# An encoder block in float32 on one Trainium2 core: 56 low parts of weights by adding transfers, and one more pair by seven products in eight stages

## Chip, core and metric

The kernel runs on one core of a Trainium2 chip. The time is the device time of that core in microseconds (us); lower is better. The other seven cores are idle.

## What is computed

One encoder layer on 256 tokens of width 2048, all in float32: a norm, one wide input projection, two kinds of attention, a gate for each, an output projection, then a gated MLP with a width-3 convolution over the tokens, then an embedding gated by the residual, and a last norm.

```python
h = rms_norm(x, attn_norm)
qa, ka, va, qb, kb, vb, ga, gb = split(h @ w_in)            # 2048 -> 10240
ya = windowed_gqa(qa, ka, va)                               # 8 heads, |i-j| <= 128, sink
yb = dilated_attention(qb, kb, vb)                          # 3 groups of 4 heads
merged = sigmoid(ga) * (ya @ w_branch_a) + sigmoid(gb) * (yb @ w_branch_b)
x = x + merged @ w_out                                      # 2048 x 2048
hf = rms_norm(x, ffn_norm)
g = dwconv(hf @ w_ffn_gate)                                 # 2048 -> 5632
x = x + (gelu(g) * (hf @ w_ffn_up)) @ w_ffn_down            # 5632 -> 2048
gate_p = sigmoid(rms_norm(x, ple_norm) @ w_ple_gate)
x = x + gate_p * (p @ w_ple_proj)
out = rms_norm(x, final_norm)
```

## The kernel before

**Numbers.** Every float32 operand is split into a high part `hi` (a copy to float32r, made by ScalarE, ACT) and a low part `lo = w - hi` (a subtraction by VectorE, DVE). A product of two operands is three matmuls on TensorE (PE): hi*hi, hi*lo, lo*hi. `thirds` issues these three (L408 to L410).

**Weights.** They come as pieces of 128 x 2048 numbers (1 MB) in the order of their use. `load` brings a piece into one of three buffers `raw` by SyncE's queue (SP); `produce` splits it unit by unit into `hi` and `lo`, lines L305 and L306. A unit is mostly 128 x 1024. Units of plain weights go into a ring of six buffers `uh`/`ul`, units of weight sums into a ring of two, `vh`/`vl`. `drop` gives a buffer back when PE has used it and makes `pump` produce the next units. A scheduler then sets the order of the instructions on each engine; instructions under `keep` stay in the order in which the program gives them. Each engine works through its own row strictly in order.

**Stages behind attention.** B0 to B3 (the two gates, each followed by the branch projections ba and bb), D0 and D1 (output projection), E0 and E1 (gate and up of the MLP, one per half of its width), F00, F01, F10, F11 (down projection: first digit the half, second the columns), pp0 and pp1, G0, and G2, G3 (embedding gate). B, D, F and G0 take two chunks of 128 inputs and two blocks of 512 columns at a time. Such a piece is either of kind `s`, eight products of three matmuls (24), or of kind `S` or `Z`, seven products (21) as in Strassen's scheme (in Winograd's form). The seven need sums of weights. For `S`, three DVE operations (L295 to L297) make them in the raw buffer; for `Z` two are enough (L282, L283), since one sum was made before, during the stages E, and laid into main memory: `sum_ahead` loads the parts by GpSimd's queue (POOL, L268), adds on DVE (L271, L272) and stores (L275). The seven also need sums of the activations (`combine`, `sums_of`: five DVE operations and a split). A string per stage says the kind of each piece: `ALT` for B1 to B3, D0, D1 and (with Z for S) G0; `FIRST_GATES` for B0; `DOWN` for the halves of F. `wide_stage` (ba, bb, G2, G3) uses pieces of kind `w`, eight products each.

**Order within a seven-product piece.** Units 0 and 1 are plain (`u`), units 2 and 3 sums (`v`); PE needs unit 2 for its second product. The `v` ring has two buffers, so the sums of one such piece can be split only when PE has left those of the one before. Where two Z stand side by side, the sums of the second are made after its second unit (`behind`).

Of the kernel before, what the change touches and what calls it, by code (L numbers as in the profile page):

```python
# [16 lines left out]
P = 128  # L17
# [74 lines left out]
WIDE = 2 * T  # L92
_JOBS = _plan()
NA = len(_JOBS)
ALT = "SsSsSsSs"
DOWN = ("ZZsZsZsZsZs", "ZsZsZsZsZss")
LASTS = 30
ASK, ADD, STORE = 0, 12, 13
FIRST_GATES = "ssssSsSs"


def _ffn(half):
# [65 lines left out]
def _unit_list():  # L168

    units, of = [], []  # L170
    for p, (kind, _) in enumerate(_PIECES):
        if p == 0:
            cuts = [("n", a * P, b * P) for a, b in ((0, 1), (1, 4), (4, 7), (7, 11), (11, PIECE))]
        elif kind == "Z":
            cuts = [("n", WIDE, 2 * WIDE), ("n", 2 * WIDE, 4 * WIDE), ("T21", 0, 2 * WIDE), ("T03", 2 * WIDE, 4 * WIDE)]
        elif kind == "S":
            cuts = [("n", 0, WIDE), ("n", 2 * WIDE, 4 * WIDE), ("T13", 0, 2 * WIDE), ("T24", 2 * WIDE, 4 * WIDE)]
        else:
            cuts = [("n", 0, 2 * WIDE), ("n", 2 * WIDE, 4 * WIDE)]
# [14 lines left out]
def _encoder(ctx: ExitStack, tc, xt, pt, xrow, cols, gainrow, table, onehot, mask, ident_in, wts, out):  # L194
# [84 lines left out]
    def sums_of_weights(raw):  # L279

        q = [raw[:, i * WIDE:(i + 1) * WIDE] for i in range(4)]
        nc.vector.tensor_tensor(q[1], q[0], q[1], op=ALU.subtract)  # L282
        nc.vector.tensor_tensor(raw[:, 2 * WIDE:], raw[:, 2 * WIDE:], view(q[0], 0, (0, 2), (1, WIDE)), op=ALU.subtract)  # L283

    def produce():

        u = state["unit"]
        p, kind, a, b = _UNITS[u]
        while state["raw"] < min(p + 3, _NPIECES):
            load(state["raw"])  # L290
        raw = raws[p]
        ring = "u" if kind == "n" else "v"
        if kind == "T13":
            q = [raw[:, i * WIDE:(i + 1) * WIDE] for i in range(4)]
            nc.vector.tensor_tensor(raw[:, :2 * WIDE], raw[:, WIDE:3 * WIDE], raw[:, :2 * WIDE], op=ALU.subtract)  # L295
            nc.vector.tensor_tensor(q[2], q[2], q[0], op=ALU.subtract)
            nc.vector.tensor_tensor(q[3], q[3], q[2], op=ALU.subtract)  # L297
        behind = _PIECES[p][0] == "Z" == _PIECES[p - 1][0]
        if kind == "T21" and not behind:
            sums_of_weights(raw)  # L300
        src = raw[:, a:b]
        pool = wpool if ring == "u" else held["tok"]
        hi = pool.tile([P, b - a], FR, name=ring + "h", bufs=RINGS[ring])
        lo = pool.tile([P, b - a], FR, name=ring + "l", bufs=RINGS[ring])
        nc.scalar.activation(hi, src, AF.Copy)  # L305
        nc.vector.tensor_tensor(lo, src, hi.bitcast(F32), op=ALU.subtract)  # L306
        if behind and u == _UNITS_OF[p][1]:
            sums_of_weights(raw)
        made[u] = (hi, lo)
        state["unit"] = u + 1  # L310
        state[ring] -= 1
# [275 lines left out]
    def at(i, f, *a):  # L587

        due.setdefault(i, []).append((f, a))
# [320 lines left out]
    def sums_of(u, tag, s=None):  # L910

        tok = held["tok"]
        f = tok.tile([P, 4, P], F32, name="cmb")
        x11, x21, x12, x22 = (u[:, k, t * P:(t + 1) * P] for k in range(2) for t in range(2))
        nc.vector.tensor_tensor(f[:, 0], x21, x22, op=ALU.add)
        nc.vector.tensor_tensor(f[:, 2], x11, x21, op=ALU.subtract)
        nc.vector.tensor_tensor(f[:, 1], f[:, 0], x11, op=ALU.subtract)
        nc.vector.tensor_tensor(f[:, 3], x12, f[:, 1], op=ALU.subtract)
        if s is None:
            s = tok.tile([P, 2, 4, P], FR, name="S", tag="S%d" % tag)  # L920
        nc.scalar.activation(s[:, 0], f, AF.Copy)
        nc.vector.tensor_tensor(s[:, 1], f, s[:, 0].bitcast(F32), op=ALU.subtract)
        return s
# [36 lines left out]
        return h  # L960

    at(("B0", 3, 0), open_tok)
    for i, when in ((4, (3, 1)), (6, (3, 6)), (0, (5, 2)), (2, (7, 2))):
        at(("B0", *when), combine, "hs", hs, i, i // 2)
    rh = halved(rc[0])

    for j in range(4):

        def gated(t, n, a):
            c = held["c"][t][:, cut[n]]  # L970
            nc.vector.tensor_tensor(c, a, c, op=ALU.add)
            a = c
            nc.scalar.activation(c, a, AF.Tanh, scale=rh[:, t:t + 1])

        if j == 1:
            at(("ba1", 0, 0), combine, "merged", held["merged"], 0, 4)
        if j == 3:
            at(("B3", 2, 4), combine, "merged", held["merged"], 2, 0)
            at(("B3", 4, 4), combine, "merged", held["merged"], 4, 1)
        quads("B%d" % j, lambda k: hs[:, k, :], lambda i: combos["hs", i], gated)  # L980
        if j == 0:
            held["merged"] = big.tile([P, KC, 2 * T], FR, name="merged", tag="R1")
        c = held["c"]
        for half, (stage, y, names) in enumerate((("ba%d" % j, lambda k: ya[:, k, :], ("M1", "M6")), ("bb%d" % j, yb.get, ("M7", "M5")))):
            accs = wide_stage(stage, y, names)
            for t in range(2):
                m = c[t][:, cut[half]]
                nc.vector.scalar_tensor_tensor(m, m, 1.0, accs[t], op0=ALU.add, op1=ALU.mult)
                if half:
                    nc.vector.tensor_tensor(c[t][:, cut[0]], c[t][:, cut[0]], m, op=ALU.add)  # L990
        merged_turns("B%d" % (j + 1) if j < 3 else "D0", j, c)
# [7 lines left out]
    def residual(stage, s, moving, key, square):  # L999

        wide = slice(2 * s * WIDE, 2 * (s + 1) * WIDE)

        def finish(t, n, a):
            r = xr[:, t, cut[2 * s + n]]
            nc.vector.tensor_tensor(r, r, a, op=ALU.add)
            if n:
                nc.vector.tensor_tensor(xr[:, t, wide], xr[:, t, wide], held["c"][t], op=ALU.add)
            if n and square:
                nc.scalar.activation(held["c"][t], xr[:, t, wide], AF.Square,
                                     accum_out=held["ssq"][:, s, t:t + 1])  # L1010

        quads(stage, moving, lambda i: combos[key, i], finish)
# [127 lines left out]
    for half in range(2):  # L1140
        held["act"], held["places"] = {}, places(half)
        jobs = _ffn(half)
        joint = 0 if half else JOINT
        stage = "E%d" % half
        accs = [bank(which) for which in ("M1", "M5", "M6", "M7")[:joint]]
        if joint:
            products(stage, lambda k: hf[:, k, :], KC, accs)
        for (kind, n), a in zip(jobs, accs):
            mlp(kind, n, a)
        turns["e"] = 0  # L1150
        todo = [(p, h) for p in sevens(half) for h in range(2)]
# [12 lines left out]
        residual("F%d0" % half, 0, activation_row, "act", half)
        if half:
            pl = big.tile([P, KC, 2 * T], FR, name="pl", tag="R0")
            for pair, when in enumerate((("F11", 0, 6), ("F11", 1, 2), ("F11", 1, 5), ("F11", 2, 1))):
                at(when, rows_pair, "P22", pair, pl, 2)
            at(("F11", 2, 4), combine, "pl", pl, 0, 0)
            at(("F11", 4, 4), combine, "pl", pl, 2, 1)  # L1170
        residual("F%d1" % half, 1, activation_row, "act", half)


# [8 lines left out]
        held["rp"] = halved(rows_root())  # L1182

    at(("pp1", 0, 0), ple_root)
    at(("pp1", 0, 4), combine, "pl", pl, 4, 2)
    at(("G0", 1, 4), combine, "pl", pl, 6, 3)
    names = ("M1", "M6", "M7", "M5")

    class Rows:
# [118 lines left out]
```

## Time and profile before

| | |
|---|---|
| time of three runs, median (lowest to highest) | 1455.31 us (1454.77 to 1455.72) |
| span of the profiled execution, first to last instruction | 1453.7 us, 19747 instructions |
| busy: PE, DVE, ACT, POOL | 1442.7 (99%), 1220.8 (84%), 829.6 (57%), 73.8 us (5%) |
| DMA | 310.17 MB, mean 213 GB/s |
| mean granted TensorE clock | 0.997 |

The profiled execution has no time of its own beside its span; the median of the runs lies 1.6 us above the span. PE's matmuls overlap, so busy time says that PE was never long without one, and the distance from start to start says what one costs. A time in a row counts from the start of the span. In the rows of groups, what stands after the bar is busy time, the mean duration of one in ns, and the idle time of the engine just before.

### The profile page before, as it was taken

Reading aid. Unit: us, or ns where it says so; the run is one execution under the profiler, and the core shown is the slowest. Engines: PE = TensorE matmul, PEld = TensorE weight load, DVE = VectorE, ACT = ScalarE, POOL = GpSimd, SP = SyncE. Lnnn points to the kernel's source line nnn. Section 1 sums busy time; section 2 is a strip of 40 time slices with the busy share of each in tenths; the row PEclk is TensorE's granted clock in tenths of the full one; section 3 lists DMA queues with packets and bytes.
Section 4 is the critical chain, followed back from the end, with each engine's and each line's share of the span. In section 5 each row is a group of like instructions: output and inputs, shape, how many; then the busy total and the mean of one; then the engine's idle time right before and its main releaser. Section 6 shows DMA issues by size and latency. Waiting matters only on the chain.

```text
span 1453.7 us, 19747 instructions
## 1 busy us (share of the span) xinstructions
PE 1442.7 (99%) x7470; PEld 1234.0 (85%) x7470; DVE 1220.8 (84%) x1730; ACT 829.6 (57%) x1148; POOL 73.8 (5%) x113
## 2 busy tenths in 40 slices
PE   9999999999999999999999999999999999999997
PEld 8888888888888888888888888888888888888885
DVE  7677665679998989989877999997878799998994
ACT  7455544546555656566545566465545466555753
POOL 0000000000000000000221100000121200000000
PEclk9999999999999999999999999999999999999998
DMA  9753445435456456465767655566776765556462
GB/s 330 252 209 146 155 167 175 172 143 203 189 190 231 180 210 239 178 253 203 277 238 267 241 208 198 189 248 227 263 275 243 271 236 213 197 194 233 173 236 82
DMA packets 58522, 310.17 MB, mean 213 GB/s; under 512 B 7028, under 2 KB 12020, under 8 KB 29500
## 3 DMA queue, kind: packets, MB, share of 16 engines
q1 hardware_dynamic: 49388, 280.46, 53.1%
q0 software_dynamic: 8320, 27.27, 5.2%
q8 instruction: 58, 0.95, 0.3%
q10 hardware_dynamic: 720, 1.19, 0.2%
q14 instruction: 36, 0.29, 0.1%
HBM read 299.94 MB, written 8.95 MB: 212 GB/s over the span
## 4 chain that ended last, share of the span: by engine, by line
PE 98%; DMA 0%; issue 0%; DVE 0%; ACT 0%; SPq 0%; POOLq 0%; POOL 0%; DVEq 0%
PE bank L351 29%; PE bank L358 15%; PE bank L408 15%; PE bank L409 14%; PE bank L410 14%; PE bank L397 2%; PE bank L399 2%; PE bank L398 2%; PE bank L335 2%; PE bank L336 1%; PE bank L939 1%; PE bank L755 0%; PE bank L703 0%; PE bank L702 0%; PE bank L701 0%; DMA raw<-in_wts 0%
## 5 line engine op out<-in xcount | busy, mean ns | idle before, releaser
L305 ACT ACTIVATE uh<-raw 128x1024 fp32r<-128x1024 f32 (+2 forms) x519 | 518.1, 1010 | 297.0 <-PE bank L410 106.5
L306 DVE TENSOR_TENSOR ul<-raw,uh 128x1024 fp32r<-128x1024 f32 (+2 forms) x519 | 594.4, 1164 | 96.5 <-ACT uh L305 65.9
L351 PE MATMUL bank<-hf,uh 128*128 128x512 f32 x1408 | 336.3, 391 | 0.0
L351 PEld LDWEIGHTS bank<-hf,uh 128*128 128x128 f32 x1408 | 258.9, 188 | 50.1
L358 PEld LDWEIGHTS bank<-hf,ul 128*128 128x128 f32 x1408 | 180.4, 191 | 6.7
L358 PE MATMUL bank<-hf,ul 128*128 128x256 f32 x1408 | 182.8, 283 | 0.0
L305 ACT ACTIVATE vh<-raw 128x1024 fp32r<-128x1024 f32 x96 | 101.1, 1058 | 59.8 <-DVE raw L282 27.0
L306 DVE TENSOR_TENSOR vl<-raw,vh 128x1024 fp32r<-128x1024 f32 x96 | 116.3, 1220 | 1.1
L351 PE MATMUL bank<-hs,uh 128*128 128x512 f32 x432 | 103.6, 392 | 0.0
L351 PEld LDWEIGHTS bank<-hs,uh 128*128 128x128 f32 x432 | 79.5, 188 | 15.6
L410 PE MATMUL bank<-uh,act 128*128 128x512 f32 x218 | 84.9, 390 | 0.0
L409 PE MATMUL bank<-ul,act 128*128 128x512 f32 x218 | 84.8, 389 | 0.0
L408 PE MATMUL bank<-uh,act 128*128 128x512 f32 x218 | 84.6, 390 | 0.0
L496 ACT ACTIVATE t<-bank 128x256 f32<-128x256 f32 x122 | 45.3, 374 | 59.8 <-PE bank L358 48.7
L408 PE MATMUL bank<-uh,hs 128*128 128x512 f32 x172 | 67.4, 392 | 0.0
L410 PE MATMUL bank<-uh,hs 128*128 128x512 f32 x172 | 67.2, 391 | 0.0
L409 PE MATMUL bank<-ul,hs 128*128 128x512 f32 x172 | 67.0, 389 | 0.0
L1084 ACT ACTIVATE gw<-gw,cl 128x256 f32<-128x256 f32 x44 | 24.0, 594 | 72.2 <-DVE gw L1081 71.9
L271 DVE TENSOR_TENSOR ahead<-ahead 128x256 f32<-128x256 f32 x52 | 21.9, 422 | 46.8 <-DMA ahead<-in_wts 46.8
L268 POOL DMA_DIRECT2D ahead<-in_wts x52 | 39.0, 750 | 375.7 <-DMA ahead<-ahead 207.0
L358 PE MATMUL bank<-hs,ul 128*128 128x256 f32 x432 | 56.6, 284 | 0.0
L358 PEld LDWEIGHTS bank<-hs,ul 128*128 128x128 f32 x432 | 54.5, 191 | 1.0
(266 smaller groups left out, 2423.8 us busy)
## 6 DMA issues: line engine op xcount, KB each, us to landing
raw<-in_wts SPq DMA_DIRECT2D x225, 1024.0 KB, 4.9
ahead<-in_wts POOLq DMA_DIRECT2D x52, 384.0 KB, 5.2
raw<-in_wts SPq DMA_DIRECT2D x26, 768.0 KB, 5.1
ahead<-ahead POOLq DMA_DIRECT2D x52, 128.0 KB, 4.4
raw<-ahead SPq DMA_DIRECT2D x26, 256.0 KB, 4.9
raw<-in_wts SPq DMA_DIRECT2D x12, 512.0 KB, 7.0
xr<-in_xrow SPq DMA_DIRECT2D x4, 512.0 KB, 8.4
x<-in_xt SPq DMA_DIRECT2D x13, 128.0 KB, 6.0
```

What stands on the lines that cost most here:

```text
L268: keep(nc.gpsimd.dma_start(q, wts[p][:, :3 * WIDE].rearrange("p (q c) -> p q c", c=WIDE)[:, :, cols]))
L305: nc.scalar.activation(hi, src, AF.Copy)
L306: nc.vector.tensor_tensor(lo, src, hi.bitcast(F32), op=ALU.subtract)
L335: nc.tensor.matmul(acc, hi[:, w], m, start=first, stop=False, skip_group_check=True)
L351: nc.tensor.matmul(acc, weights(u)[0][:, o * P:(o + 1) * P], m, start=first, stop=False, skip_group_check=True)
L358: nc.tensor.matmul(acc[:, T:], weights(u)[1][:, o * P:(o + 1) * P], m[:, :T], start=False, stop=last, skip_group_check=True)
L397: nc.tensor.matmul(acc[:, :n * P], xh, hi, start=(k == 0), stop=False)
L398: nc.tensor.matmul(acc[:, :n * P], xh, lo, start=False, stop=False)
L408: nc.tensor.matmul(acc, sh, wh, start=first, stop=False)
L409: nc.tensor.matmul(acc, sh, wl, start=False, stop=False)
L410: nc.tensor.matmul(acc, sl, wh, start=False, stop=last)
L496: keep(nc.scalar.activation(t, acc[:, T:], AF.Copy, scale=scale))
```

## The change

**Low parts by adding transfers.** `_MOVED` is a set of 56 units: the second unit of each piece of kind `s` or `w` in B, ba, bb, D, F and G0 (27 in B, ba and bb, 6 in D, 20 in F, 3 in G0). For them ACT makes two copies, `-hi` into the low buffer and `hi`; then a transfer issued by POOL reads the same 512 KB of weights from main memory once more and adds them to the low buffer. The DVE subtraction falls away. The transfer is under `keep`.

**One more pair by seven products** in each of B1, B2, B3, D0, D1, G0, F10 and F11, by the strings. Some pieces by seven now stand side by side (`SS`, `ZZ`), and `behind` holds for S too. B0 keeps two, at later places. `combine` is asked for one more pair in each of hs, merged and pl, at new places, and the added sums get a buffer `act2`. G0's third Z and F1's sixth make six more sums ahead, 34 in E1 where there were 28.

```diff
-ALT = "SsSsSsSs"
-DOWN = ("ZZsZsZsZsZs", "ZsZsZsZsZss")
+ALT = "SsSSsSSs"
+DOWN = ("ZZsZsZsZsZs", "ZZsZsZsZsZs")
-FIRST_GATES = "ssssSsSs"
+FIRST_GATES = "sssssSSs"
...
+_MOVED = {_UNITS_OF[p][1] for stage in _STAGES if stage[0] in "BbDFG" and stage not in ("G2", "G3")
+          for p in _STAGES[stage] if _PIECES[p][0] in 'sw'}
...
-        if kind == "T13":
-            q = [raw[:, i * WIDE:(i + 1) * WIDE] for i in range(4)]
-            ...
-        behind = _PIECES[p][0] == "Z" == _PIECES[p - 1][0]
+        behind = _PIECES[p][0] in "SZ" and _PIECES[p - 1][0] in "SZ"
+        if kind == "T13" and not behind:
+            all_sums_of_weights(raw)
...
-        nc.scalar.activation(hi, src, AF.Copy)
-        nc.vector.tensor_tensor(lo, src, hi.bitcast(F32), op=ALU.subtract)
+        if u in _MOVED:
+            nc.scalar.activation(lo, src, AF.Copy, scale=-1.0)
+            nc.scalar.activation(hi, src, AF.Copy)
+            keep(nc.gpsimd.dma_start(lo, wts[p][:, a:b], accum_op=ALU.add))
+        else:
+            nc.scalar.activation(hi, src, AF.Copy)
+            nc.vector.tensor_tensor(lo, src, hi.bitcast(F32), op=ALU.subtract)
         if behind and u == _UNITS_OF[p][1]:
-            sums_of_weights(raw)
+            (sums_of_weights if _PIECES[p][0] == "Z" else all_sums_of_weights)(raw)
...
-    for i, when in ((4, (3, 1)), (6, (3, 6)), (0, (5, 2)), (2, (7, 2))):
-        at(("B0", *when), combine, "hs", hs, i, i // 2)
+    for i, when, tag in ((5, (3, 6), 2), (6, (4, 5), 3), (0, (5, 5), 0), (2, (6, 5), 1), (3, (7, 2), 5)):
+        at(("B0", *when), combine, "hs", hs, i, tag)
```

In the built program PE has 24 matmuls of 128x512 fewer. How the rows stand at the places that matter, the numbers behind a name telling one buffer from another:

ACT near the start of F01, before: the second unit of the fourth piece (an `s`), which PE uses against `act1`, is `uh_8631`; it stands behind the sums `vh_8615` of the Z ahead of it.

```order
L305 ACTIVATE vh_8549<-raw_8405 128x1024
L305 ACTIVATE uh_8590<-raw_8481 128x1024
L305 ACTIVATE vh_8561<-raw_8405 128x1024
L305 ACTIVATE vh_8605<-raw_8481 128x1024
L305 ACTIVATE uh_8621<-raw_8565 128x1024
L305 ACTIVATE vh_8615<-raw_8481 128x1024
L305 ACTIVATE uh_8631<-raw_8565 128x1024
L305 ACTIVATE uh_8663<-raw_8575 128x512
```

The same place now: the second unit of that piece is `uh_8730`, and its negative copy `ul_8731`, on which the adding transfer waits, stands one row further back.

```order
L316 ACTIVATE vh_8647<-raw_8502 128x1024
L316 ACTIVATE uh_8689<-raw_8579 128x1024
L316 ACTIVATE vh_8659<-raw_8502 128x1024
L312 ACTIVATE ul_8670<-raw_8544 128x1024
L316 ACTIVATE vh_8704<-raw_8579 128x1024
L316 ACTIVATE vh_8714<-raw_8579 128x1024
L316 ACTIVATE uh_8720<-raw_8663 128x1024
L313 ACTIVATE uh_8730<-raw_8663 128x1024
L312 ACTIVATE ul_8731<-raw_8663 128x1024
```

So the transfer can start only behind both copies, which both stand behind the sums `vh_8714` of the Z.

DVE at the end of E1, before: rows of L500 gather E1's products out of the PSUM banks (the last three are `bank_11252`, `bank_11314` and `bank_11361`), which F10's products then take; L282 and L283 make the sums of F10's first Z (`raw_11172`), L306 splits weights.

```order
L282 TENSOR_TENSOR raw_11172<-raw_11172 128x512
L283 TENSOR_TENSOR raw_11172<-raw_11172 128x1024
L1092 SCALAR_TENSOR_TENSOR gw_11143<-gw_11143 128x512
L500 TENSOR_TENSOR pair_11191<-bank_11252,t_11306 128x256
L306 TENSOR_TENSOR vl_11299<-raw_11172,vh_11298 128x1024
L306 TENSOR_TENSOR vl_11303<-raw_11172,vh_11302 128x1024
L1101 SCALAR_TENSOR_TENSOR pair_11191<-pair_11191,rms_5806 128x512
L306 TENSOR_TENSOR ul_11342<-raw_11220,uh_11341 128x1024
L1102 TENSOR_TENSOR pair_11191<-pair_11191,gw_10933 128x512
L306 TENSOR_TENSOR ul_11354<-raw_11220,uh_11353 128x1024
L1111 TENSOR_TENSOR act1_11311<-pair_11191,act1_11311 128x2x256
L500 TENSOR_TENSOR pair_11357<-bank_11314,t_11358 128x256
```

The same place now; the last three products are `bank_11387`, `bank_11459` and `bank_11509`, F10's first Z is `raw_11301` and its second `raw_11354`:

```order
L284 TENSOR_TENSOR raw_11301<-raw_11301 128x512
L285 TENSOR_TENSOR raw_11301<-raw_11301 128x1024
L1104 SCALAR_TENSOR_TENSOR gw_11272<-gw_11272 128x512
L317 TENSOR_TENSOR vl_11433<-raw_11301,vh_11432 128x1024
L317 TENSOR_TENSOR vl_11437<-raw_11301,vh_11436 128x1024
L273 TENSOR_TENSOR ahead_11328<-ahead_11328 128x256
L511 TENSOR_TENSOR pair_11323<-bank_11387,t_11443 128x256
L274 TENSOR_TENSOR ahead_11328<-ahead_11328 128x256
L1113 SCALAR_TENSOR_TENSOR pair_11323<-pair_11323,rms_5899 128x512
L317 TENSOR_TENSOR ul_11488<-raw_11354,uh_11487 128x512
L1114 TENSOR_TENSOR pair_11323<-pair_11323,gw_11059 128x512
L317 TENSOR_TENSOR ul_11500<-raw_11354,uh_11499 128x1024
```

The gather of the third last product stood ahead of the splits of the Z's sums; now it stands behind them and behind an addition for a sum ahead (L273), which waits for a load. From there to the gather of the next product it is 14 rows, where it was 7: the second Z's splits and sums and the sums of one pair of activations.

POOL before, behind attention: nothing but two norms until the sums ahead of E0.

```order
L528 TENSOR_TENSOR rr_595<-rv_593,mhalf_78 128x4
L528 TENSOR_TENSOR rr_5757<-rv_5755,mhalf_78 128x2
L268 DMA ahead_5996<-in_wts 128x3x256
L268 DMA ahead_6045<-in_wts 128x3x256
L275 DMA ahead152_5995<-ahead_5996 128x256
L268 DMA ahead_6098<-in_wts 128x3x256
```

POOL now, at the end of E1: the last sums ahead, and right behind them the adding transfers for F10.

```order
L277 DMA ahead247_11014<-ahead_11114 128x256
L270 DMA ahead_11228<-in_wts 128x3x256
L277 DMA ahead248_11227<-ahead_11228 128x256
L270 DMA ahead_11328<-in_wts 128x3x256
L277 DMA ahead248_11227<-ahead_11328 128x256
L314 DMA ul_11586<-in_wts 128x1024
L314 DMA ul_11647<-in_wts 128x1024
L314 DMA ul_11727<-in_wts 128x1024
```

All 33 adding transfers of the stages B and D stand on POOL in front of its first load for a sum ahead; in F no other work stands between them.

More of the change, by code (lines that the diff above doesn't have):

```diff
@@ L283, in sums_of_weights, with all_sums_of_weights @@
         nc.vector.tensor_tensor(raw[:, 2 * WIDE:], raw[:, 2 * WIDE:], view(q[0], 0, (0, 2), (1, WIDE)), op=ALU.subtract)
+    def all_sums_of_weights(raw):
+        q = [raw[:, i * WIDE:(i + 1) * WIDE] for i in range(4)]
+        nc.vector.tensor_tensor(raw[:, :2 * WIDE], raw[:, WIDE:3 * WIDE], raw[:, :2 * WIDE], op=ALU.subtract)
+        nc.vector.tensor_tensor(q[2], q[2], q[0], op=ALU.subtract)
+        nc.vector.tensor_tensor(q[3], q[3], q[2], op=ALU.subtract)
     def produce():
@@ L292, in produce @@
         ring = "u" if kind == "n" else "v"
-        if kind == "T13":
-            q = [raw[:, i * WIDE:(i + 1) * WIDE] for i in range(4)]
-            nc.vector.tensor_tensor(raw[:, :2 * WIDE], raw[:, WIDE:3 * WIDE], raw[:, :2 * WIDE], op=ALU.subtract)
-            nc.vector.tensor_tensor(q[2], q[2], q[0], op=ALU.subtract)
-            nc.vector.tensor_tensor(q[3], q[3], q[2], op=ALU.subtract)
-        behind = _PIECES[p][0] == "Z" == _PIECES[p - 1][0]
+        behind = _PIECES[p][0] in "SZ" and _PIECES[p - 1][0] in "SZ"
+        if kind == "T13" and not behind:
+            all_sums_of_weights(raw)
         if kind == "T21" and not behind:
@@ L919, in sums_of @@
         if s is None:
-            s = tok.tile([P, 2, 4, P], FR, name="S", tag="S%d" % tag)
+            s = tok.tile([P, 2, 4, P], FR, name="S", tag="S%d" % tag if tag < 5 else "act2")
         nc.scalar.activation(s[:, 0], f, AF.Copy)
@@ L978, in _encoder @@
             at(("B3", 2, 4), combine, "merged", held["merged"], 2, 0)
-            at(("B3", 4, 4), combine, "merged", held["merged"], 4, 1)
+            at(("B3", 4, 4), combine, "merged", held["merged"], 3, 1)
+            at(("B3", 7, 4), combine, "merged", held["merged"], 5, 5)
         quads("B%d" % j, lambda k: hs[:, k, :], lambda i: combos["hs", i], gated)
@@ L1170, in _encoder @@
             at(("F11", 4, 4), combine, "pl", pl, 2, 1)
+            at(("F11", 6, 4), combine, "pl", pl, 3, 2)
         residual("F%d1" % half, 1, activation_row, "act", half)
@@ L1184, in _encoder @@
     at(("pp1", 0, 0), ple_root)
-    at(("pp1", 0, 4), combine, "pl", pl, 4, 2)
-    at(("G0", 1, 4), combine, "pl", pl, 6, 3)
+    at(("pp1", 0, 4), combine, "pl", pl, 5, 3)
+    at(("G0", 1, 4), combine, "pl", pl, 6, 4)
     names = ("M1", "M6", "M7", "M5")
```

## The prediction

> **What bounds the kernel now.** I read the page first: the busy line, the chain that ended last and the DMA rate in forty slices.
>
> ```profile
> PE 1442.7 (99%) x7470; PEld 1234.0 (85%) x7470; DVE 1220.8 (84%) x1730; ACT 829.6 (57%) x1148; POOL 73.8 (5%) x113
> PE 98%; DMA 0%; issue 0%; DVE 0%; ACT 0%; SPq 0%; POOLq 0%; POOL 0%; DVEq 0%
> GB/s 330 252 209 146 155 167 175 172 143 203 189 190 231 180 210 239 178 253 203 277 238 267 241 208 198 189 248 227 263 275 243 271 236 213 197 194 233 173 236 82
> ```
>
> PE carries the whole chain, so only two things change the time: matmuls taken away, and matmuls that come to wait. The waits say how many wait now (total us, count, largest).
>
> ```profile
> PE bank L234 <- DVE mhalf L229: 1.1, 1, 1.1
> PE bank L336 <- DVE ul L306: 0.2, 1, 0.2
> ACT uh L305 <- DMA raw<-in_wts: 41.5, 35, 3.0
> DVE ahead L271 <- DMA ahead<-in_wts: 46.8, 25, 3.3
> POOL ahead L268 <- DMA ahead<-ahead: 207.0, 48, 5.6
> ```
>
> PE's two waits come to 1.3 us. There is no stall that relief of DVE could give back: what DVE saves is worth nothing by itself, what PE loses counts in full. ACT already waits for 35 weight loads, DVE for 25 loads of the sums ahead. The windows by stage show the room that is left (window, us, PE, PE load, DVE, ACT, POOL busy with counts, clock, DMA share, GB/s): B1, D0, D1, F01.
>
> ```profile
> 367.00:425.00 58.00, 58.00 (x261) 47.95 (x260) 54.07 (x65) 34.31 (x38) 0.00 (x0) 1.00 0.53 195
> 542.00:585.00 43.00, 43.00 (x194) 35.25 (x193) 41.74 (x51) 26.92 (x29) 0.00 (x0) 1.00 0.68 248
> 585.00:627.00 42.00, 42.00 (x189) 33.42 (x189) 40.28 (x49) 25.59 (x33) 0.00 (x0) 1.00 0.52 193
> 930.00:987.00 57.00, 57.00 (x252) 46.78 (x251) 54.08 (x58) 31.37 (x34) 0.00 (x0) 1.00 0.61 226
> ```
>
> DVE is busy 93 to 97% of these stages though 84% overall, ACT some 60%. So the change relieves the engine that is nearly full, in the right stages; its price is paid in latency and DMA traffic.
>
> **The change, part by part.** *24 matmuls less.* Two matmuls twelve apart stand 2.75 us apart, 0.229 us each.
>
> ```profile
> 1295.45 0.39 PE L408 MATMUL bank<-uh,act 128*128 128x512 f32 x1
> 1298.20 0.39 PE L408 MATMUL bank<-vh,S 128*128 128x512 f32 x1
> ```
>
> 24 x 0.229 = **-5.5 us**, all on the path. This is the floor: nothing else shortens PE's row.
>
> *Busy time of DVE, ACT and POOL.* The durations are those of the groups:
>
> ```profile
> L306 DVE TENSOR_TENSOR ul<-raw,uh 128x1024 fp32r<-128x1024 f32 x466 | 560.9, 1220 | 81.6 <-ACT uh L305 51.4 <-PE bank L358 15.5 <-issue 13.7
> L305 ACT ACTIVATE uh<-raw 128x1024 fp32r<-128x1024 f32 x466 | 486.0, 1054 | 236.0 <-PE bank L351 80.8 <-PE bank L410 71.8 <-DMA raw<-in_wts 39.1
> L306 DVE TENSOR_TENSOR ul<-raw,uh 128x512 fp32r<-128x512 f32 x49 | 33.7, 687 | 12.7 <-ACT uh L305 12.4
> L283 DVE TENSOR_TENSOR raw<-raw 128x1024 f32<-128x1024 f32 x26 | 31.7, 1220 | 0.2
> L282 DVE TENSOR_TENSOR raw<-raw 128x512 f32<-128x512 f32 x26 | 17.9, 687 | 0.2
> L295 DVE TENSOR_TENSOR raw<-raw 128x1024 f32<-128x1024 f32 x22 | 26.9, 1222 | 0.3
> L296 DVE TENSOR_TENSOR raw<-raw 128x512 f32<-128x512 f32 x22 | 15.1, 685 | 0.0
> L918 DVE TENSOR_TENSOR cmb<-pair,cmb 128x128 f32<-128x128 f32 x23 | 6.6, 285 | 0.1
> L922 DVE TENSOR_TENSOR S<-cmb,S 128x512 fp32r<-128x512 f32 x16 | 11.0, 685 | 0.0
> L268 POOL DMA_DIRECT2D ahead<-in_wts x52 | 39.0, 750 | 375.7 <-DMA ahead<-ahead 207.0 <-PE bank L410 168.7
> L271 DVE TENSOR_TENSOR ahead<-ahead 128x256 f32<-128x256 f32 x52 | 21.9, 422 | 46.8 <-DMA ahead<-in_wts 46.8
> ```
>
> DVE loses 56 x 1.22 = 68 us. A new S adds splits of 0.69 + 1.22 and sums of 1.22 + 2 x 0.685, 4.5 us; a new Z the same splits and sums of 0.69 + 1.22, 3.8 us; five S and three Z make 34. Four more combinations are 4 x (5 x 0.285 + 0.685) = 8, six more sums ahead 6 x 2 x 0.422 = 5. DVE stands 21 us better over the whole. ACT gets 56 x 1.05 = 59 us, covered by its 236 us of idle time ahead of these copies; POOL 56 x 0.75 = 42, covered since it has nothing else there. The place where that cover fails is the latency of single units.
>
> *Latency of a moved low part, F.* Before, the low part is ready one subtraction (1.22 us) behind the copy. Now it is ready one more copy and one transfer later. No row shows an adding transfer. The nearest are POOL's own loads (KB, median us to landing), and the spread of a tile's landings (weights, then sums ahead):
>
> ```profile
> raw<-in_wts SPq DMA_DIRECT2D x225, 1024.0 KB, 4.9
> ahead<-in_wts POOLq DMA_DIRECT2D x52, 384.0 KB, 5.2
> ahead<-ahead POOLq DMA_DIRECT2D x52, 128.0 KB, 4.4
> DMA to landing us min/median/max: 2.7/5.0/8.9
> DMA to landing us min/median/max: 3.3/4.8/6.5
> ```
>
> POOL's two sizes give 0.8 us for 256 KB, so 5.6 us for 512 KB as a plain load and 7.2 if the target is read as well, like 1 MB. I take the middle, 6.4 us; the ends are 3.3 (POOL's fastest) and 8.9 (the slowest of all). How much lead there is now, from the copy to the first matmul that takes its low part, I followed unit by unit behind attention. Most have 8 us and more. The tight ones, one each in F00, F01 and F11, are the second unit of a plain piece behind the sums of a Z (copies of ACT, then PE; the first copy of a row ends 1.04 us after its start):
>
> ```profile
> 889.57 2.52 ACT L305 ACTIVATE uh<-raw 128x1024 fp32r<-128x1024 f32 x3
> 895.54 0.39 PE L409 MATMUL bank<-ul,act 128*128 128x512 f32 x1
> 947.07 2.51 ACT L305 ACTIVATE uh<-raw 128x1024 fp32r<-128x1024 f32 x3
> 951.63 0.39 PE L409 MATMUL bank<-ul,act 128*128 128x512 f32 x1
> 1310.16 2.51 ACT L305 ACTIVATE uh<-raw 128x1024 fp32r<-128x1024 f32 x3
> 1315.70 0.39 PE L409 MATMUL bank<-ul,act 128*128 128x512 f32 x1
> ```
>
> Leads 4.93, 3.52 and 4.50 us. The extra copy takes 0.95 (three copies start within 2.5 us), which leaves 3.98, 2.57 and 3.55. At 6.4 the low parts come 2.4, 3.8 and 2.9 us late: **+9**. At 3.3 only F01's does, 0.7: +1; at 8.9 it is 4.9 + 6.3 + 5.4: +17. The order agrees that nothing was pulled forward: in F01 the copy that the transfer waits for still stands behind the sums `vh_8714`.
>
> The Trainium skill ("DMA: Bandwidth & Descriptors", "Anatomy of one DMA — SWDGE (gpsimd) path") fits a transfer issued from GpSimd by 2.0 us + bytes/436e3, an estimate of 3.2 us for 512 KB, and the F term would be under 1 us. The same formula gives 2.9 us for the 384 KB load, where this trace has 5.2, so in this loaded kernel the trace disagrees with it.
>
> *Start of F10, by E1's last gathers.* PE needs the banks that E1's last products leave. The last gather and the first matmul in the bank it frees:
>
> ```profile
> 1234.73 0.42 DVE L500 TENSOR_TENSOR pair<-bank,t 128x256 f32<-128x256 f32 x1
> 1235.78 0.39 PE L408 MATMUL bank<-uh,S 128*128 128x512 f32 x1
> ```
>
> It ends at 1235.15, 0.63 us before its use. In the new order seven more DVE rows stand between the last gathers (0.4 to 1.22 each, some 6 us), and an addition for a sum ahead stands in front, which waits 1.9 us in the mean (46.8/25), 3.3 at most. Behind it, in DVE's row, wait gathers, and PE behind those. The bounds are 0, if DVE, relieved, runs that far ahead, and 6 + 1.9 - 0.6 = 7. I take **+4**, the middle.
>
> *D0 and D1.* DVE was busy 41.74 + 40.28 = 82.0 of 85 us. Two more S add 9.0, one combination 2, six moved units take 7.3: 85.7 at most and 83.7 if the combination falls ahead of D, against 85 - 1.4 of PE. No slack is left, and any wait of DVE shows: 0 to 4, **+2**.
>
> *B and G0.* Here the leads are long, for example in B0 (the second copy ends at 337.06, use at 346.09: 9.03 us):
>
> ```profile
> 335.07 1.99 ACT L305 ACTIVATE uh<-raw 128x1024 fp32r<-128x1024 f32 x2
> 346.09 0.39 PE L409 MATMUL bank<-ul,hs 128*128 128x512 f32 x1
> ```
>
> A transfer of 6.4 us fits. 27 of 0.52 MB in 238 us add 59 GB/s to B1's 195, which is about what stages with no stall of PE move (D0, 248). What remains is S beside S: the second one's sums (2.6 us of DVE) start only behind its second unit, and its splits only when PE leaves the first one's. Four such pairs at 0 to 2.6 us, one late low part in G0: 0 to 12, **+4**.
>
> **Sum**: -5.5 + 9 + 4 + 2 + 4 = +13.5 on the span of 1453.7: 1467.2. The runs' median lies 1.6 above the span, so 1469.
>
> **Rivals.** *A, the adding transfer is far dearer.* If reading, adding and writing take twice a plain transfer, 11 us, then even the B0 lead of 9.03, less 0.95, is short by 2.9. For the 20 units of F I take 2 us each, since one late unit gives the next one time: 40 in place of 9. That makes +44.5, 1500 in the runs. For it: POOL's loads land late even now, and D0 would go from 248 GB/s to 248 + 2 x 3 x 0.52 MB/43 us = 321, near the page's highest slice (330), so ACT's 35 waits for weights grow too. Against it: main memory is read only once per unit; the other operand lies in the core.
>
> The Trainium skill ("Collectives: The Full Stack", "The bandwidth ceiling: the fold count and why AG ≠ RS ≠ AR") says that a reducing transfer needs two source reads and measured 1.93 times a copy. By this the transfer would be nearer A than the 6.4 us above. No row of this trace holds such a transfer.
>
> *B, everything is hidden: faster.* If a transfer lands in 3.5 us or less, or DVE's 21 us pull the sums of the Z's forward so that copies start some 3 us earlier in F, and E1's gathers still come in time, only -5.5 remains: 1448.2 + 1.6 = 1449.8. For it: DVE is the fullest engine beside PE in exactly these stages, and in F01 alone loses 5 x 1.22 = 6.1 of 54.08 us. Against it: the median of POOL's 384 KB loads is already 5.2. It decides at an adding latency of about 3.5 us: under it this rival wins, over it the F term begins to eat the gain.
>
> *C, transfers in time, only DVE's order costs.* Then -5.5 + 4 + 2 = +0.5: 1455.8.
>
> **How the numbers follow.** Late low parts and starts (the sum): 0.45, its own range 1460 to 1486 (terms at low and high ends, not all at once). A 0.18, B 0.25, C 0.12. 0.2% is 2.9 us, about what a measurement here can tell from none. Faster is B, 0.25; same 0.07, most of C; slower 0.45 + 0.18 + 0.05 = 0.68. The range 1449 to 1505 takes in B and the middle of A and leaves out A's upper part and a little of B, under 2 in 10.
>
> **What the profile afterwards would show.** PE's matmuls 24 fewer. In the waits, PE behind an adding transfer in F00, F01 and F11, 2 to 4 us each; PE behind DVE's gathers (L511) at F10's start, some 4 us. The landing median of the adding transfers between 5.6 and 7.2 us. DVE some 21 us less busy, ACT some 60 more, the DMA 29 MB more. The forecast is wrong if PE's waits stay near 1 us (B), or if low parts come late in most pieces of F and in B too (A).

## The result and the profile after

The changed kernel takes 1595.09 us (three runs, 1594.08 to 1596.49) against 1455.31: ratio 1.0959, 95% interval 1.0939 to 1.0979, 140 us slower. The forecast was slower, 1469 in a range to 1505. The way was right, the size wrong by a factor of ten.

The page of the kernel after, busy line and chain that ended last:

```profile
PE 1488.4 (93%) x7446; PEld 1255.0 (79%) x7446; DVE 1203.6 (76%) x1747; ACT 892.3 (56%) x1225; POOL 130.3 (8%) x181
PE 67%; DMA 19%; issue 6%; ACT 4%; DVE 3%; POOL 0%; POOLq 0%; ACTq 0%; DVEq 0%
```

PE has its 24 matmuls less (7446 for 7470) and is yet busy 45.7 us longer; and it is idle 1593.3 - 1488.4 = 104.9 us, where it was 11.0. So the span of 1593.3 is longer by 93.9 us of idle and 45.7 of busy time, and since 24 matmuls fell away (5.5), the others took 51 us more. DVE is 17 us less busy, ACT 63 more. In the chain the adding transfer (`ul<-in_wts`) is the largest entry of DMA, 13 of its 19%. The waits of PE (total us, count, longest) and the DMA issues (KB, median us to landing):

```profile
PE bank L420 <- DMA ul<-in_wts: 76.8, 28, 6.3
PE bank L419 <- DVE c L903: 7.2, 2, 3.7
PE bank L419 <- DVE pair L511: 5.8, 2, 3.3
raw<-in_wts SPq DMA_DIRECT2D x222, 1024.0 KB, 5.2
raw<-in_wts SPq DMA_DIRECT2D x29, 768.0 KB, 6.6
ul<-in_wts POOLq DMA_DIRECT2D x56, 512.0 KB, 9.5
ahead<-in_wts POOLq DMA_DIRECT2D x58, 384.0 KB, 5.2
```

The adding transfer lands after 9.5 us. The 1 MB loads beside it go from 4.9 to 5.2 us, those of 768 KB from 5.1 to 6.6; the loads for the sums ahead keep 5.2. PE waits for the adding transfer 28 times: 9 in B, 5 in D, 11 in F, 3 in G0. Where the time goes is seen from windows by groups of stages: B and D, E0, F00 and F01, E1, and the rest, before and then after (window, us, PE, PE load, DVE, ACT, POOL, clock, DMA share, GB/s).

```profile
304.00:627.50 323.50, 323.50 (x1462) 265.82 (x1461) 303.52 (x376) 189.77 (x220) 0.00 (x0) 1.00 0.54 197
627.50:874.70 247.20, 247.20 (x1428) 218.50 (x1428) 209.30 (x344) 143.53 (x215) 32.63 (x49) 1.00 0.67 241
874.70:986.70 112.00, 112.00 (x493) 92.03 (x493) 105.28 (x115) 62.91 (x70) 0.00 (x0) 1.00 0.57 211
986.70:1231.70 245.00, 245.00 (x1410) 216.54 (x1410) 204.40 (x331) 136.74 (x201) 37.03 (x56) 1.00 0.69 246
1231.70:1453.00 221.30, 212.27 (x952) 175.07 (x950) 190.78 (x248) 128.66 (x176) 2.93 (x3) 0.98 0.52 189
```

```profile
304.00:679.60 375.60, 339.28 (x1443) 270.98 (x1442) 296.51 (x385) 223.19 (x264) 27.01 (x31) 0.95 0.71 218
679.60:927.20 247.60, 247.60 (x1428) 218.59 (x1428) 206.97 (x341) 143.56 (x215) 32.55 (x49) 1.00 0.66 236
927.20:1058.90 131.70, 119.60 (x494) 95.81 (x492) 93.45 (x103) 72.99 (x80) 8.69 (x10) 0.95 0.71 217
1058.90:1304.00 245.10, 245.03 (x1409) 216.61 (x1410) 202.51 (x335) 131.75 (x195) 44.41 (x67) 1.00 0.72 257
1304.00:1593.00 289.00, 233.99 (x943) 186.50 (x941) 198.28 (x269) 150.94 (x204) 14.48 (x17) 0.90 0.54 171
```

E0 and E1, which have no moved unit, take as long as before, though E1 moves bytes at the highest rate of all. B and D lose 52 us, F00 and F01 20, the rest 68. In every group that loses, the granted clock is below the 1.00 (or 0.98, in the rest) of before. One wait in G0 shows both halves of the loss: ACT's negative copy, the transfer in the chain, then PE's row.

```profile
1478.60 1.13 ACT L312 ACTIVATE ul<-raw 128x1024 fp32r<-128x1024 f32 x1
1480.14 11.30 DMA ul<-in_wts
1484.78 0.39 PE L419 MATMUL bank<-uh,pl 128*128 128x512 f32 x1
1491.47 0.79 PE L420 MATMUL bank<-ul,pl 128*128 128x512 f32 x1 [6.31 <-DMA ul<-in_wts]
1492.07 0.63 PE L421 MATMUL bank<-uh,pl 128*128 128x512 f32 x1
1492.49 0.63 PE L419 MATMUL bank<-uh,pl 128*128 128x512 f32 x1
...
1496.33 0.63 PE L419 MATMUL bank<-uh,pl 128*128 128x512 f32 x1
1496.76 0.58 PE L420 MATMUL bank<-ul,pl 128*128 128x512 f32 x1
```

PE is idle for 6.3 us, and the matmuls behind the wait start 0.427 us apart instead of 0.229: eleven from 1492.07 to 1496.76 take 4.7 us where 2.5 would do. The record of the granted clock (the third number from the end in these windows, 0.50 and then 1.00) has a stretch at half clock just there:

```profile
1490.30:1497.10 6.80, 5.62 (x13) 4.45 (x14) 2.52 (x6) 0.00 (x0) 0.00 (x0) 0.50 0.43 155
1497.10:1514.20 17.10, 12.97 (x57) 10.32 (x55) 11.88 (x14) 10.54 (x12) 0.87 (x1) 1.00 0.49 143
```

The trace has 20 such stretches before PE's last microseconds, of 3.4 or 6.8 us. Each of them follows an idle time of PE of 1.9 us or more, and each idle time of 2.5 us or more (there are 17) has one. The matmuls in them make up some 40 of the 51 us. In the kernel before, where PE never waited for more than 1.1 us, there is no such stretch ahead of the end.

### The profile page after: what moved, and what is told of

It is laid out like the page before. It is cut to its first block, busy times and chain, and to the rows that moved or that the text cites. A ratio compares the mean times of both kernels' runs of the same rounds, so it can differ in the third digit from the quotient of the medians.

```text
span 1593.3 us, 19994 instructions
## 1 busy us (share of the span) xinstructions
PE 1488.4 (93%) x7446; PEld 1255.0 (79%) x7446; DVE 1203.6 (76%) x1747; ACT 892.3 (56%) x1225; POOL 130.3 (8%) x181
## 4 chain that ended last, share of the span: by engine, by line
PE 67%; DMA 19%; issue 6%; ACT 4%; DVE 3%; POOL 0%; POOLq 0%; ACTq 0%; DVEq 0%
PE bank L362 25%; DMA ul<-in_wts 13%; PE bank L369 13%; PE bank L420 7%; PE bank L421 6%; PE bank L419 6%; DMA raw<-in_wts 4%; PE bank L346 2%; PE bank L408 2%; PE bank L410 2%; PE bank L409 2%; ACT vh L316 1%; DVE ul L317 1%; DMA ahead<-in_wts 1%; PE bank L347 1%
## 5 line engine op out<-in xcount | busy, mean ns | idle before, releaser
L317 DVE TENSOR_TENSOR ul<-raw,uh 128x1024 fp32r<-128x1024 f32 (+2 forms) x463 | 525.5, 1149 | 195.1 <-ACT uh L316 165.7
L316 ACT ACTIVATE uh<-raw 128x1024 fp32r<-128x1024 f32 (+2 forms) x463 | 457.1, 998 | 365.8 <-PE bank L421 137.2
L317 DVE TENSOR_TENSOR vl<-raw,vh 128x1024 fp32r<-128x1024 f32 x112 | 136.1, 1221 | 22.5 <-ACT vh L316 21.1
L316 ACT ACTIVATE vh<-raw 128x1024 fp32r<-128x1024 f32 x112 | 117.4, 1052 | 40.9 <-PE bank L421 13.5
L314 POOL DMA_DIRECT2D ul<-in_wts x56 | 49.0, 874 | 925.8 <-ACT ul L312 353.4
L420 PE MATMUL bank<-ul,act 128*128 128x512 f32 x208 | 88.3, 425 | 29.4 <-DMA ul<-in_wts 29.3
L420 PEld LDWEIGHTS bank<-ul,act 128*128 128x128 f32 x208 | 42.2, 203 | 43.0 <-DMA ul<-in_wts 34.2
L420 PE MATMUL bank<-ul,hs 128*128 128x512 f32 x154 | 63.0, 409 | 13.4 <-DMA ul<-in_wts 13.4
L270 POOL DMA_DIRECT2D ahead<-in_wts x58 | 43.5, 750 | 243.2 <-DMA ahead<-ahead 227.8
L419 PE MATMUL bank<-uh,hs 128*128 128x512 f32 x154 | 62.4, 405 | 0.0
L421 PE MATMUL bank<-uh,hs 128*128 128x512 f32 x154 | 62.1, 403 | 0.0
L273 DVE TENSOR_TENSOR ahead<-ahead 128x256 f32<-128x256 f32 x58 | 24.5, 422 | 49.3 <-DMA ahead<-in_wts 49.2
```

Of the source, the lines that this page charges most:

```text
L270: keep(nc.gpsimd.dma_start(q, wts[p][:, :3 * WIDE].rearrange("p (q c) -> p q c", c=WIDE)[:, :, cols]))
L314: keep(nc.gpsimd.dma_start(lo, wts[p][:, a:b], accum_op=ALU.add))
L419: nc.tensor.matmul(acc, sh, wh, start=first, stop=False)
L420: nc.tensor.matmul(acc, sh, wl, start=False, stop=False)
L421: nc.tensor.matmul(acc, sl, wh, start=False, stop=last)
```

## The experiments

The theory (T, later L): the low part of a moved unit is ready only behind ACT's copies, the issue and the landing in a row, and this row is longer than the time until PE wants it. The main rivals: DVE's new order and the new pairs (D); the queue or the traffic, with any transfer (Q). For the single units I followed each issue to its landing and to the moment at which PE would have wanted the low part: the start of the matmul ahead of the first one that takes it, plus 0.229 us. The time from the issue to that moment is called the lead.

### The pairs without the transfers

```diff
-_MOVED = {_UNITS_OF[p][1] for stage in _STAGES if ...}
+_MOVED = set()
```

> Keeps the one more pair by seven products in eight stages, but every low part is again a subtraction on DVE. Theory T (the adding transfers land late, and PE waits for them): nearly all of the +140 us goes; what stays is -5.5 us of matmuls and up to +15 of DVE's extra rows (sums, splits, combinations), 1450 to 1468 us. Rival D (the order of DVE and S beside S make the loss, the transfers only show as the last to come): 1500 us or more, with PE waiting for low parts and sums of DVE in B, D and F.

1477.76 us, ratio 1.0148 (1.0122 to 1.0174). So 118 of the 140 us go with the transfers; D is refused as the main cause, but the pairs are no gain either: +22, above the 1468 I allowed. PE's waits, the longest of the whole kernel, then those in D alone (557 to 651 us):

```profile
PE bank L418 <- DVE pair L510: 6.2, 2, 4.8
PE bank L418 <- ACT vh L315: 4.8, 6, 2.7
PE bank L361 <- DVE hf L523: 1.3, 1, 1.3
PE bank L419 <- DVE vl L316: 0.9, 1, 0.9
```

The first row is the start of F10, the others D0 and D1. In B, 304 to 557 us, PE waits for nothing: S beside S is hidden there. PE's busy line is 1448.9 us in a span of 1475.4, so it is idle for 26.5 us, 15.5 more than before; its matmuls are 6.2 us longer in all though 24 are gone. That makes the 22.

### The transfers without the pairs

The edit of `produce` with the rule of `_MOVED`, put into the kernel before.

> The strings, combinations and sums of the kernel before; only the low parts move, by the same rule, which with these strings picks 64 units in place of 56. Theory T: as slow as the changed kernel or slower by 8/56 of its loss, 1580 to 1620 us, PE behind adding transfers some 30 times. Rival D: under 1480 us, since DVE is relieved by 78 us and gets nothing new.

1558.51 us, ratio 1.0708 (1.0692 to 1.0724), with 64 transfers. They cost 103 us without any new pair, less than I expected and far above D's bound of 1480. PE's wait and the transfer:

```profile
PE bank L416 <- DMA ul<-in_wts: 58.3, 24, 6.9
ul<-in_wts POOLq DMA_DIRECT2D x64, 512.0 KB, 9.3
```

22 and 103 make 125 of the 140, and the 103 are of 64 transfers, not 56: the two parts together cost a little more than each alone.

### A plain transfer in place of the adding one

```diff
-keep(nc.gpsimd.dma_start(lo, wts[p][:, a:b], accum_op=ALU.add))
+keep(nc.gpsimd.dma_start(lo, wts[p][:, a:b]))
```

> The changed kernel in the same order, but the transfer writes its 512 KB over the low buffer and does not add (so the low parts are wrong numbers: the weights themselves). Theory T1 (adding makes the transfer slow, about twice the work of a plain one for the DMA engines): median landing 5.2 to 6.4 us in place of 9.5, PE waits under 25 us in all, 1465 to 1490 us. Rival Q (any transfer of POOL is that late behind the 1 MB loads of SP's queue): landing stays at 8.5 to 10 us and the time within 1% of 1595.

The low buffer now holds the weights themselves; the subtraction of `hi` is left out. 1529.59 us, ratio 1.0515 (1.0491 to 1.0540), the same order of instructions. Both expectations fail in the time: landing is what T1 said, 6.2 us, yet the time is 52 us above the pairs alone.

```profile
PE bank L420 <- DMA ul<-in_wts: 34.7, 19, 5.1
ul<-in_wts POOLq DMA_DIRECT2D x56, 512.0 KB, 6.2
```

So adding makes the transfer slow, 66 us of the loss, but a plain one put in the same place is too late as well: 14 of its 56 leads are shorter than 6.4 us, and the landings go up to 10.2. The 19 late ones are 4 in B, 4 in D, 9 in F and 2 in G0. The DMA engines' time says how much work an adding transfer is. The software queue of the pairs alone, of this kernel and of the changed one:

```profile
q0 software_dynamic: 9280, 30.42, 5.6%
q0 software_dynamic: 17344, 59.78, 11.8%
q0 software_dynamic: 17344, 59.78, 15.2%
```

As shares of spans of 1475.4, 1528.4 and 1593.3 us these are 83, 180 and 242 us, so 56 plain transfers take 98 and 56 adding ones 160: 1.6 times, though the bytes are counted once. The Trainium skill ("Collectives: The Full Stack", "The bandwidth ceiling: the fold count and why AG ≠ RS ≠ AR") has two source reads and a ratio of 1.93 for the reducing collective beside the copying one, in a ring of several cores; the trace of this one core agrees in kind, with a smaller ratio.

### The same without ACT ahead of it

```diff
-nc.scalar.activation(lo, src, AF.Copy, scale=-1.0)
```

on top of the plain transfer. The low buffer holds the weights themselves, as above.

> As the kernel with the plain transfer (1529.6 us), and without ACT's negative copy: the transfer waits for nothing but the low buffer, and starts earlier by ACT's place in the row and one copy (the low parts are wrong numbers, the weights themselves). Theory L (what PE waits for is the sum of copies, issue and landing against a lead of some 8 us that PE's own use of the ring sets): PE's 34.7 us of waits for transfers fall under 10, 1475 to 1500 us, near the 1477.8 of the pairs alone. Rival (the transfers slow the loads of weights, and PE waits for those in any case): 1515 to 1530 us.

1474.28 us, ratio 1.0138 (1.0121 to 1.0154). All 55 us are gone, 0.7 us below the range I gave, with the same 56 transfers and the same bytes; no wait of PE is put down to a transfer, and the two longest are these:

```profile
PE bank L418 <- DVE pair L510: 6.1, 2, 4.1
PE bank L418 <- DVE c L902: 4.7, 3, 2.2
ul<-in_wts POOLq DMA_DIRECT2D x56, 512.0 KB, 5.1
```

So POOL's queue and 29 MB more cost no time that shows as long as the transfers start early (DVE has 57 us less to do here than with the pairs alone, 1201.4 for 1258.3, and that gains nothing that shows either: the four runs of the pairs alone spread from 1471 to 1481). Q is refused as a cause by itself. But a transfer beside more traffic takes longer: of these 56, the 14 with the least bytes of SP's queue in the 5 us behind their issue land after 4.0 us in the median, the 14 with the most after 7.4. Here the leads cover that.

### Adding onto zeros

```diff
-nc.scalar.activation(lo, src, AF.Copy, scale=-1.0)
+nc.gpsimd.memset(lo.bitcast(F32), 0.0)
```

Again the low buffer ends with the weights themselves, now by an adding transfer that waits for nothing of ACT.

> The fourth of a square: the transfer adds, as in the changed kernel, but onto zeros that POOL writes into the low buffer as soon as it is free, in place of ACT's negative copy (so the low parts are wrong numbers, the weights themselves); nothing of ACT stands ahead of the transfer. The other three: plain and without ACT 1474.3, plain behind ACT 1529.6, adding behind ACT 1595.1. If the loss is the queue of ACT's copy and transfer against one lead: the 9.5 us landing starts early enough for most units, 1478 to 1505 us. If the adding transfer costs 65 us whenever it starts: 1530 to 1550 us.

1497.14 us, ratio 1.0284 (1.0267 to 1.0302), inside the range of the theory.

```profile
PE bank L420 <- DMA ul<-in_wts: 10.1, 4, 6.1
ul<-in_wts POOLq DMA_DIRECT2D x56, 512.0 KB, 7.3
```

This closes the square; lead and landing are medians, the last column counts the waits and sums what came later than PE's want:

| transfer | time | lead | landing | late |
|---|---|---|---|---|
| plain, nothing of ACT ahead | 1474.3 | 11.1 | 5.1 | none |
| adding, nothing of ACT ahead | 1497.1 | 10.4 | 7.3 | 4, 11 us |
| plain, behind ACT's copy | 1529.6 | 8.1 | 6.2 | 19, 38 us |
| adding, behind ACT's copy | 1595.1 | 9.0 | 9.5 | 28, 82 us |

Adding alone costs 23 us, standing behind ACT alone 55, both together 121: each takes from the same lead, and what is over counts. The leads in the changed kernel go from 3.1 to 14.3 us. That the landing itself is 7.3 in one and 9.5 in the other goes at least in part with SP's traffic: onto zeros, the 14 transfers with the least of it in the 5 us behind their issue land after 5.6 us in the median, the 14 with the most after 10.0, and behind ACT's copy a transfer meets more (1.05 MB in the median, for 0.88). Whether that is all of it was not tested.

### ACT's copies alone

```diff
-keep(nc.gpsimd.dma_start(lo, wts[p][:, a:b], accum_op=ALU.add))
+nc.vector.tensor_tensor(lo, src, hi.bitcast(F32), op=ALU.subtract)
```

> The pairs alone, low parts by DVE as before, but ACT makes the 56 negative copies all the same (into the low buffer, where DVE's subtraction then overwrites them). Theory L (ACT's work costs only where a transfer and PE queue behind it): within 8 us of the pairs alone (1477.8), 1472 to 1486 us. Rival (59 us more on ACT delay the copies of all units, and that is what PE waits for): 1500 us or more, PE behind ACT's copies.

1480.35 us, ratio 1.0173 (1.0157 to 1.0188): 2.6 us above the pairs alone. ACT's 59 us are covered, as predicted; they became dear only where a transfer stood behind them.

### Only the units that came in time

> The changed kernel, but only the 27 units move whose transfer came in time in it; the 29 late ones are subtracted on DVE again. If lateness is a matter of the single unit's lead: no more waits than a few us, 1450 to 1475 us. If those 27 came in time only because PE had just been held up by a neighbour: a good part of them is late now, some 10 to 15 waits of 1 to 4 us, 1500 to 1540 us.

1521.59 us, ratio 1.0465 (1.0439 to 1.0490).

```profile
PE bank L421 <- DMA ul<-in_wts: 34.0, 12, 5.7
```

Of 27 units that had been in time 12 are now late. All 12 have shorter leads than in the changed kernel (3.7 to 9.0 us, where it was 7.6 to 13.4), and for 7 of them PE had stood still within the lead there, so these had been saved by waits just ahead of them. For the other five the cause is open. A trace of a stalled kernel doesn't tell which transfers are harmless.

### Later use within a piece

```diff
-t, n, c = g // 4, g // 2 % 2, g % 2
+c, t, n = (g // 4, g // 2 % 2, g % 2) if 0 < i < len(pieces) - 1 else (g % 2, g // 4, g // 2 % 2)
...
```

In the middle of a stage `c`, the unit, now changes last, and the first unit's buffers are given back after its four products.

> The changed kernel, but in plain pieces of kind s in the middle of a stage PE makes the four products of the first unit and then the four of the second, in place of turn about; so the second unit's low part is wanted three products (9 matmuls, 2.06 us) later, and the first unit's buffers come free earlier. Theory L: about half of the 29 late transfers gain 2 us and more, with the slow matmuls behind them, 1540 to 1570 us. Rival (lateness moves with PE, so that a unit that is given time only starts later): 1585 to 1600 us.

1576.13 us, ratio 1.0831 (1.0816 to 1.0845): 19 us better, between the expectations. PE waits 59.7 us for transfers, 28 times as before. Most of the 2 us are lost again: the median lead is 9.3 us, where it was 9.0. That the whole chain of copies moves with PE would explain it, but was not shown by itself.

### Halves of 256 KB

Each adding transfer is issued as two, one for each half of the low buffer.

> The changed kernel with each adding transfer cut into two of 256 KB, the half that PE wants first sent first. If the time of an adding transfer goes by its bytes: the first half lands some 6.5 to 7.5 us after its issue, the second some 10, which PE wants 1.4 us after the first; PE's waits for transfers fall by a third or more, 1530 to 1560 us. Rival (a fixed delay of some 9 us, whatever the size): landing of both stays near 9 us, 1585 to 1610 us.

1603.17 us, ratio 1.1005 (1.0986 to 1.1023): the rival's case.

```profile
ul<-in_wts POOLq DMA_DIRECT2D x112, 256.0 KB, 8.6
```

The 8.6 mixes two kinds: the first halves land after 7.8 us in the median, the second ones, issued 0.5 us behind them, after 9.7, and a pair is complete 10.4 us after its first issue, where one whole transfer took 9.5. The two halves are under way together, so this run doesn't show what a transfer of 256 KB alone would take, and a fixed delay is not shown. It shows that cutting the transfer gains nothing.

### Filling the waits of PE

```diff
 nc.tensor.matmul(acc, sh, wh, start=first, stop=False)
+for _ in range(_FILL.pop(u, 0)):
+    nc.tensor.matmul(acc[:32], zero, wh, start=False, stop=False)
...
```

> The changed kernel with 237 matmuls that add zeros (32 columns of a zero tile by 512), 54 us of PE, put where PE waited over 1.7 us for a transfer, just ahead of the waiting matmul, so that each wait is left with some 0.9 us. Theory C (a wait of over 2 us lets the granted clock fall, and the matmuls behind it run at half speed for some 2 us): the slow matmuls' 38 us nearly vanish, 1555 to 1570 us in spite of 237 matmuls more. Rival (they are slow for the transfers' traffic, not for the wait): 1595 us, with matmuls of 0.43 us start to start in the same places.

1571.63 us, ratio 1.0792 (1.0778 to 1.0807): 237 matmuls more, 23 us less, though 1.6 us above the range I gave. The clock is 0.987 where it was 0.967. The busy line and PE's two largest groups of waits:

```profile
PE 1514.3 (96%) x7683; PEld 1263.0 (80%) x7683; DVE 1205.7 (77%) x1747; ACT 891.1 (57%) x1226; POOL 130.3 (8%) x181
PE bank L425 <- DMA ul<-in_wts: 18.1, 16, 3.5
PE bank L422 <- DVE c L908: 11.1, 2, 5.9
```

Without the fill's 54.3 us (237 x 0.229) PE is busy 1460.0, 28 less than in the changed kernel. So more than half of the 51 us of slower matmuls comes from the waits as such. The clock's record accounts for some 14 us more: 7 stretches at half clock are left of the 20, behind idle times of 2.0 to 5.9 us (3.5 at most for a transfer, 5.9 for DVE's `c`). The last 9 us were not settled, and the fill changed the order too. The Trainium skill ("TensorE: Matmul & The Clock Gate", "Part 1: The HAM clock gate (the "warmup" mystery)") gives half rate after an idle window of about 3.4 us and full rate after a busy one. The 0.427 us start to start and the stretches of 3.4 and 6.8 us agree with it; but in the changed kernel an idle time of 1.9 us was once enough, and each of 2.5 and more, so the 3.4 us are no safe limit here.

### Low parts on POOL

```diff
-nc.scalar.activation(lo, src, AF.Copy, scale=-1.0)
 nc.scalar.activation(hi, src, AF.Copy)
-keep(nc.gpsimd.dma_start(lo, wts[p][:, a:b], accum_op=ALU.add))
+nc.gpsimd.tensor_tensor(lo, src, hi.bitcast(F32), op=ALU.subtract)
```

for the moved units, in place of the negative copy and the transfer.

> The changed kernel, its 56 low parts neither by transfers nor on DVE but as a subtraction on POOL, behind ACT's one copy. Theory L: the low part is ready one POOL operation behind the copy; if that takes 2 to 4 us, the leads of 3.5 us and more hold it, PE's waits for transfers are gone, DVE keeps its 68 us of relief, and the time is that of the pairs alone (1477.8) or better, 1455 to 1480 us. Rival (POOL's subtraction takes over 6 us, or DVE's own operations slow down beside it): 1500 us or more, with PE behind POOL or DVE.

1550.26 us, ratio 1.0653 (1.0635 to 1.0671): the rival. The groups of POOL and DVE, and PE's waits for them:

```profile
L313 POOL TENSOR_TENSOR ul<-raw,uh 128x1024 fp32r<-128x1024 f32 x56 | 187.0, 3341 | 776.4 <-ACT uh L312 444.8 <-PE bank L368 302.2 <-PE bank L420 14.8
L316 DVE TENSOR_TENSOR vl<-raw,vh 128x1024 fp32r<-128x1024 f32 x112 | 151.1, 1360 | 11.7 <-ACT vh L315 10.7
L316 DVE TENSOR_TENSOR ul<-raw,uh 128x512 fp32r<-128x512 f32 x57 | 57.4, 1007 | 14.4 <-ACT uh L315 14.1
PE bank L419 <- DVE vl L316: 23.3, 18, 2.8
PE bank L419 <- POOL ul L313: 5.1, 1, 5.1
```

POOL takes 3.34 us in the mean, and PE waits for it once. But DVE's subtractions of 128x512, 687 ns before, now take 1007 in the mean: the 16 of the 57 that overlap a subtraction on POOL take 1832, the other 41 take 685. DVE's busy time is 1281.5 us for the same 1747 instructions that took 1203.6, and above the 1258.3 of the pairs alone, where DVE made the 56 low parts itself: what POOL takes over, DVE loses beside it.

### A pair more in B alone

The strings and combinations of B, without transfers and with D, F and G0 as before.

> The kernel before with one more pair by seven products in B1, B2 and B3 alone (B0's two at their later places, S beside S), no transfers, nothing new in D, F and G0. In the run of the pairs alone PE had no wait in B. If that holds: 9 matmuls less, -2.06 us, 1453.2 us (ratio 0.9986). Rival (the sums of S beside S or of hs at new places come late when the rest of the order is another): 1456 to 1462 us.

1457.42 us, ratio 1.0014 (1.0005 to 1.0023): the rival's side, 2 us slower for 9 matmuls less. Its profile has short waits in D, whose pieces are unchanged but whose order is not, and 5.0 us in E1 that belong to that single run (1464.46 us, the others 1457.0 to 1458.1). The cause of the 2 us was not settled. No version here beats the kernel before.

## Why the prediction was wrong

- *Latency of a moved low part, 6.4 us:* this step failed first. The landing is 9.5 us in the median, above the upper end of 8.9 that I took from the slowest load. The rows were all of plain transfers; no row bounds a kind of transfer that the kernel never made. Plain, in the same place, it was 6.2, near the 6.4. The fit of the Trainium skill ("DMA: Bandwidth & Descriptors", "Anatomy of one DMA — SWDGE (gpsimd) path"), 3.2 us, was reached by none: the fastest of the 56 plain transfers without ACT took 3.8.
- *The tight units, one each in F00, F01 and F11 (+9):* this step failed with it, and by itself too. "Most have 8 us and more" doesn't cover 9.5: 28 of 56 were late, 9 of them in B, where I had written that the transfer fits, and 5 in D, whose leads I had not priced. But the count of three was wrong even for the latency that I had assumed: with the plain transfer, which landed after 6.2, 19 units were late and the time was 52 us above the pairs alone. Of these 19, 13 had a lead under 6.4 us; the other six were late by landings longer than the median, which the sum put at nothing. The count of late units is a threshold in the latency, and the sum treated it as a slope: the bound of 17 kept the count at three.
- *What PE loses counts in full:* it counted more than in full. To 94 us of idle time came 51 of slower matmuls, some 40 of them in stretches at half clock behind PE's waits. No term had this; before, PE never stood long enough to show it.
- *B and G0, +4:* more traffic cost no time by itself, as I had put it (the plain transfer without ACT shows this), though it lengthened landings; S beside S was hidden in B, and the leads were the error.
- *Start of F10, +4:* right within its bounds of 0 to 7, with 5.8 us of waits for the gathers (6.2 with the pairs alone). *D, +2:* too small, 7.0 us of waits with the pairs alone, above the 4 that I allowed. The terms without transfers, -5.5 + 4 + 2 + 4, make +4.5, where the pairs alone cost 22: -5.5, 15.5 of idle time and 12 of slower matmuls.
- *Busy times:* DVE -21 (measured -17), ACT +60 (+63), both covered, as costed; DVE's relief was worth nothing, as said.
- *Rival A* had the mechanism, a dear adding transfer (11 us, measured 9.5), and 0.18. Its sign, low parts late in B too, came true. It missed the size, 1500, since it priced 20 units at 2 us, left B and D out, and had no clock. *Rival B* fell with the landing. *C*, all transfers in time, was not this kernel's case; where they were in time (plain, without ACT) the time was 1474, not 1456.
- The way, slower, was no luck: late low parts were what made the +9. The size was off because most of the late ones, and the clock, were not in the sum.

## What to carry to other kernels

A step that moves from an engine to a transfer is to be compared with the lead of every unit, not with the busy share of the engine relieved: here an operation of 1.22 us became a row of copies, issue and landing of some 11 us (10.9 in the median from the start of the negative copy to the landing), and half the low parts came later than PE wanted them. Where the price of an unseen operation decides by a threshold, work out the result at twice the price for all units before settling on the middle. A wait of PE of 2 us and more is to be priced above its length: in this kernel the matmuls behind such waits ran at half clock for 3.4 or 6.8 us at a time.

## What the hardware showed that I had not expected

An adding transfer of 512 KB took 1.6 times a plain one's time of the DMA engines and landed after 9.5 us; onto zeros, with nothing of ACT ahead, after 7.3. The landings went with the bytes that SP's queue moved beside them: 4.0 us among few and 7.4 among many for the plain transfer without ACT. A wait of 6.3 us was followed by matmuls of 0.427 us start to start, and the clock's record shows half clock behind idle times of PE from 1.9 us up. DVE's 128x512 subtractions took 1832 ns where they overlapped a subtraction on POOL and 685 where they didn't; the Trainium skill ("SBUF — State Buffer", "Who interferes with whom") says that a DVE instruction with two inputs in SBUF contends with a GpSimd instruction that reads it, and that run agrees.
